# Two fused transformer blocks on one core: 128 weight loads issued by GpSimd in place of SyncE

## The chip, the cores and the metric

The kernel runs on one core of a Trainium2 chip, as one launch. Its time is the device time in microseconds (us) of that launch, the median of several runs. The core has five engines that matter here: TensorE (PE, matrix products, with its weight loads as PEld), VectorE (DVE), ScalarE (ACT), GpSimd (POOL) and SyncE (SP). Each engine carries out its own instructions in the order in which they stand in its stream, and an instruction at the head that waits holds back all that stand behind it. Sixteen DMA engines move data between the device memory and the on-chip memory; a transfer is issued by an instruction on one of the engines.

## The reference

Two transformer blocks on 256 tokens of width 2048 and batch 1, in f32. What this case touches is the first block's modulation: six vectors of 2048 numbers that come from one condition vector by one large weight matrix, `w_ada` (2048 x 12288 f32, 100.7 MB).

```python
cond = jax.nn.silu(c)
mod = cond @ w_ada[i] + b_ada[i]
shift1, scale1, gate1, shift2, scale2, gate2 = jnp.split(mod, N_MOD, axis=-1)
h = _modulate(_rms(x, norm1_w[i]), shift1, scale1).astype(x.dtype)
u, q, k, v = jnp.split(h @ w_in[i], splits, axis=-1)
y_ssm = _s5_mixer(u, ...)              # a scan over 256 steps, gelu, a gate
y_att = _dilated_attention(q, k, v, q_norm_w[i], k_norm_w[i])
mixed = jnp.concatenate([y_ssm, y_att], axis=-1) @ w_out[i]
x = x + gate1[:, None, :] * mixed
h2 = _modulate(_rms(x, norm2_w[i]), shift2, scale2).astype(x.dtype)
ffn = (jax.nn.silu(h2 @ w_ffn_gate[i]) * (h2 @ w_ffn_up[i])) @ w_ffn_down[i]
x = x + gate2[:, None, :] * ffn
```

A second block of another kind follows, with its own modulation weights (`ada_w_2`), attention over a context, and a layer that mixes by Fourier transforms. The change touches none of it.

## The kernel before, in words

**Weights as tiles of 512 KB.** Nearly all work is to stream weights past 256 tokens. A weight tile is 128 partitions x 2 x 512 f32 (512 KB), loaded into a buffer of the tag `raw`, of which there are five (`NRAW`). For a product, ACT writes the tile's upper part (`wh`, L177), DVE the rest (`wl<-raw,wh`, L178), three buffers each, and PE does three products for one: 12 matmuls for one tile of 256 weight rows, two token halves at a time (the "k2 step" of `gemm`). After each step `tick()` lets the side lanes go on.

**The lane `ada`.** The modulation is a vector times a matrix, done beside the rest by a generator, `ada_all`. A tile is loaded into a `raw` buffer, and DVE adds the tile times one condition value per partition to an accumulator (`acc<-raw,condT,acc`, L278, 128 x 1024). In order: the first gate (`row`, 32 tiles), the second shift and second scale (`cols1`, each 16 tiles through DVE by `ada_gen` and 16 through PE by `ada_quad`, which takes the raw tile itself as the moving operand), then the second gate (`row` again, 32 tiles), and after that the second block's vectors from `ada_w_2`. `ada_gen` issues its loads at L306, `ada_quad` at L353. The first block's first shift and scale come earlier, from another function with its own loads at L742 (64 of them), which no change concerns.

**What sets the order.** The lane's pace is given by hand (`rate["ada"]`), and `until("g1")`, `until("m2")`, `until("g2")` make it reach a point. In the feed-forward part:

```python
    rate["ada"] = 0.5                      # L1114: one lane step for two k2 steps
        if np_ == 0:
            lanes["ada"].until("g2")       # L1147: after the first half of the FFN
```

The program order is then rearranged per engine by the Tile framework's scheduler, which also decides which of the five `raw` buffers a tile gets and puts in the waits: a load waits until its buffer's last reader is done. All 192 loads of `w_ada` are SP instructions, as are the loads of the products' weights (L214, and L207 for tiles that PE uses unsplit); they stand in one stream and go through one hardware queue, q1. POOL has 12 memsets and no load.

Of the kernel before, what the change touches and what calls it, by code (L numbers as in the profile page):

```python
# [81 lines left out]
def kernel(ctx: ExitStack, tc: tile.TileContext, A, out):  # L82
    nc = tc.nc
    V, S, G, PE, SY = nc.vector, nc.scalar, nc.gpsimd, nc.tensor, nc.sync
# [14 lines left out]
    def uname(s):  # L99
        count[0] += 1  # L100
        return f"{s}_{count[0]}"
# [30 lines left out]
    def mm(o, l, r, start, stop):  # L132
        PE.matmul(o, l, r, start=start, stop=stop)  # L133
# [23 lines left out]
    def rsqrt(src, scale, shape, key="r"):  # L157

        w, y, t, yi = (small(shape, key + n, d) for n, d in (("w", F32), ("y", F32), ("t", F32), ("i", I32)))
        V.tensor_scalar(out=w, in0=src, scalar1=float(scale), scalar2=EPS, op0=ALU.mult, op1=ALU.add)  # L160
        V.tensor_scalar(out=yi, in0=w.bitcast(I32), scalar1=1, scalar2=None, op0=ALU.logical_shift_right)
        V.tensor_scalar(out=yi, in0=yi, scalar1=-1, scalar2=0x5F3759DF, op0=ALU.mult, op1=ALU.add)
        V.tensor_scalar(out=w, in0=w, scalar1=-0.5, scalar2=None, op0=ALU.mult)
        y0 = yi.bitcast(F32)
        for i in range(3):
            if shape[1] == 1:
                V.tensor_scalar(out=t, in0=y0, scalar1=y0, scalar2=w, op0=ALU.mult, op1=ALU.mult)
                V.tensor_scalar(out=y, in0=t, scalar1=1.5, scalar2=y0, op0=ALU.add, op1=ALU.mult)
            else:
                V.tensor_tensor(out=t, in0=y0, in1=y0, op=ALU.mult)  # L170
                V.tensor_tensor(out=t, in0=t, in1=w, op=ALU.mult)
                V.scalar_tensor_tensor(out=y, in0=t, scalar=1.5, in1=y0, op0=ALU.add, op1=ALU.mult)
            y0 = y
        return y
# [98 lines left out]
    def ada_add(acc, raw, vec, kk, first=False):  # L273
        c = condT[:, vec + kk:vec + kk + 1]
        if first:
            V.tensor_scalar(out=acc, in0=raw, scalar1=c, scalar2=None, op0=ALU.mult)
        else:
            V.scalar_tensor_tensor(out=acc, in0=raw, scalar=c, in1=acc, op0=ALU.mult, op1=ALU.add)  # L278
# [7 lines left out]
    def zipped(*gens):  # L286

        gens = list(gens)
        while gens:
            for g in list(gens):  # L290
                try:
                    yield next(g)
                except StopIteration:
                    gens.remove(g)

    def ada_gen(W, bc, col0, vecs, accs, row=False):

        bc = bc + col0 // 128
        if row:
            for j in range(8):  # L300
                S.activation(out=accs[0][:, j * 128:(j + 1) * 128], in_=ident, func=AF.Copy,
                             scale=bcol[:, bc + j:bc + j + 1])
        for kk in range(ND):
            raw = wp.tile([128, 2, 512], F32, name=uname("raw"), tag="raw", bufs=NRAW)
            rf = raw.rearrange("p k n -> p (k n)")
            SY.dma_start(rf, W[kk * 128:(kk + 1) * 128, col0:col0 + 1024])  # L306
            for a, v in zip(accs, vecs):
                ada_add(a, rf, v, kk, kk == 0 and not row)
            yield 1.0
# [37 lines left out]
    def ada_quad(b, W, r, c0, n, last):  # L347

        m = 1024 // n
        raws = []  # L350
        for q in range(0, 4, m):
            raw = wp.tile([128, m, n], F32, name=uname("raw"), tag="raw", bufs=NRAW)
            SY.dma_start(raw, W[(r + q) * 128:(r + q + m) * 128, c0:c0 + n].rearrange("(k p) n -> p k n", p=128))  # L353
            raws.append(raw)
            yield 1.0
        for j in range(4):
            mm(b[32 * j:32 * j + 32, 0:n], cz[:, r + j], raws[j // m][:, j % m], r == 0, last)

    def ada_pe(W, i, chunks, dst, add, mul=None):

        for c in chunks:
            b = ps_mm()
            for r in range(0, ND, 4):
                yield from ada_quad(b, W, r, i * D + c * 512, 512, r == ND - 4)
            cols = ada_turn(b, 512, 128)
            o = dst[:, c * 4:c * 4 + 4]
            bc = i * ND + c * 4
            V.tensor_reduce(out=o, in_=cols, axis=AX.X, op=ALU.add)
            V.scalar_tensor_tensor(out=o, in0=o, scalar=float(add), in1=bcol[:, bc:bc + 4], op0=ALU.add, op1=ALU.add)
            if mul is not None:  # L370
                V.tensor_tensor(out=o, in0=o, in1=colv[:, mul + c * 4:mul + c * 4 + 4], op=ALU.mult)
# [8 lines left out]
    w_ada = A["w_ada"][0]  # L380
    aw = A["ada_w_2"]

    def ada_all():
        def cols(W, bc, i, v, dst, add):

            accs = [ada_acc() for _ in range(2)]
            yield from zipped(*(ada_gen(W, bc, i * D + h * 1024, [v], [accs[h]]) for h in range(2)))
            ada_cols(accs, [(dst, 8 * h, bc + i * ND + 8 * h) for h in range(2)], add)

        def row(W, bc, i, v, dst):  # L390
            dst += [None] * 2
            accs = [ada_acc() for _ in range(2)]
            yield from zipped(*(ada_gen(W, bc, i * D + h * 1024, [v], [accs[h]], True) for h in range(2)))
            ada_row(accs, dst)

        def half(W, i, dst, add, mul):
            acc = ada_acc()
            yield from ada_gen(W, 0, i * D, [C_C], [acc])
            ada_cols([acc], [(dst, 0, i * ND)], add, mul)
# [432 lines left out]
    r = rsqrt(s1, 1.0 / D, [128, 2])  # L832
# [5 lines left out]
    for c0 in range(0, ND, 2):  # L838
        b = ps_tp()
        for c in range(2):  # L840
            for t in range(2):
                o = (c * 2 + t) * 128
                k = c0 + c
# [187 lines left out]
    for nt in range(4):  # L1031
        ps = gemm([(z, 0), (z, 1)], w_out, 0, 8, nt * 512, 512, stagger=3 * (nt == 3))
        for t in range(2):
# [8 lines left out]
            if nt == 3:  # L1042
                s1 = small([128, 1], "s1")
                V.tensor_reduce(out=s1, in_=ssq[t], axis=AX.X, op=ALU.add)
                r = rsqrt(s1, 1.0 / D, [128, 1])
# [689 lines left out]
```

## Time and profile before

| | |
|---|---|
| median of 3 runs | 2492.14 us (2489.64, 2492.14, 2492.82) |
| the profiled execution | 2486.17 us |
| its span, first to last instruction | 2484.4 us |
| mean granted TensorE clock | 0.983 |
| PE, DVE, ACT, POOL busy | 95%, 73%, 45%, 0% |
| memory traffic | 587.19 MB read, 237 GB/s over the span |
| loads of `w_ada`: L742, L306, L353 | 64, 96, 32, of 512 KB |
| their time in the span | L742 4.9 to 180.5 us, L306 191.7 to 707.0 us, L353 290.8 to 524.6 us |

The table is read in this way: PE is busy for nearly all of the span, so that another engine or a transfer costs time only where it makes PE wait. The stretch that holds loads of L306 and L353 goes from 191.7 to 707.0 us. In it lie the projections of the first block with its scan and attention (to about 453 us), the output projection and the second norm (to about 552 us), and that part of the feed-forward products beside which the second gate's tiles are loaded (to about 712 us).

### The profile page before, as it was taken

How to read it: one execution, taken by the hardware profiler on the slowest of the kernel's cores; microseconds unless marked ns; L12 is line 12 of the kernel's file. 1: busy time of each engine (PE TensorE's matmuls, PEld its weight loads, DVE VectorE, ACT ScalarE, POOL GpSimd, SP SyncE). 2: the span in 40 equal slices, each digit the busy share in tenths (PEclk: the TensorE clock that was granted, in tenths of full speed). 3: DMA queues.
4: the chain of work that ended last, by engine and by line, in shares of the span. 5: the costliest groups of instructions: out<-in, count | busy, mean ns of one | idle time of the engine just before them, and what ended most of it. 6: DMA issues, size and time to landing. Idle time of an engine off the chain costs nothing.

```text
span 2484.4 us, 30494 instructions
## 1 busy us (share of the span) xinstructions
PE 2352.2 (95%) x10855; PEld 1800.0 (72%) x10855; DVE 1810.1 (73%) x3054; ACT 1124.0 (45%) x1745; POOL 1.4 (0%) x12
## 2 busy tenths in 40 slices
PE   5899999989999999999999999999997999999997
PEld 3455554668887878778777888777776778888886
DVE  5877998787778899876778789646678655555557
ACT  3227752454444333344355455555435445444442
POOL 0000000000000000000000000000000000000000
PEclk9899999999999999999999999999998999999999
DMA  9888778768888878888877988624473765665664
GB/s 290 309 296 307 231 260 285 253 224 291 286 278 273 297 267 291 266 270 280 266 250 222 306 282 291 210 89 162 136 262 115 231 200 176 193 194 157 177 210 138
DMA packets 291538, 591.35 MB, mean 238 GB/s; under 512 B 33733, under 2 KB 56617, under 8 KB 291385
## 3 DMA queue, kind: packets, MB, share of 16 engines
q1 hardware_dynamic: 291384, 589.40, 73.1%
q8 instruction: 85, 1.39, 0.2%
q14 instruction: 69, 0.56, 0.1%
HBM read 587.19 MB, written 2.13 MB: 237 GB/s over the span
## 4 chain that ended last, share of the span: by engine, by line
PE 47%; DMA 22%; DVE 20%; issue 5%; ACT 4%; SPq 1%; DVEq 0%; ACTq 0%
PE mm L133 39%; DMA raw<-in_ada_w_dram 15%; DVE wl L178 6%; DVE acc L278 6%; PE at L133 4%; PE tp L133 2%; DMA raw<-in_w_in_attn_dram 2%; DMA raw<-in_w_ada_dram 2%; ACT ssm_us L663 1%; ACT wh L177 1%; DMA raw<-in_w_ffn_down_dram 1%; PE tp L189 1%; DVE ssm_h L684 1%; DVE ssm_tq L682 1%; DVE wa L278 1%
## 5 line engine op out<-in xcount | busy, mean ns | idle before, releaser
L133 PE MATMUL mm<-wh,s 128*128 128x512 f32 (+3 forms) x4768 | 1462.9, 386 | 2.3 <-ACT wh L177 2.1
L177 ACT CAST wh<-raw 128x1024 fp32r<-128x1024 f32 (+3 forms) x642 | 655.9, 1023 | 896.8 <-PE mm L133 669.9
L133 PEld LDWEIGHTS mm<-wh,s 128*128 128x128 f32 x4768 | 890.2, 189 | 181.1 <-issue 7.8
L178 DVE TENSOR_TENSOR wl<-raw,wh 128x1024 fp32r<-128x1024 f32 (+3 forms) x642 | 755.2, 1185 | 316.6 <-ACT wh L177 311.9
L133 PE MATMUL mm<-wl,s 128*128 128x512 f32 (+3 forms) x2384 | 920.4, 386 | 21.4 <-DVE wl L178 19.6
L278 DVE SCALAR_TENSOR_TENSOR acc<-raw,condT,acc 128x1024 f32<-128x1024 f32 (+2 forms) x413 | 477.7, 1164 | 208.8 <-DMA raw<-in_ada_w_dram 141.9
L133 PEld LDWEIGHTS mm<-wl,s 128*128 128x128 f32 x2384 | 450.5, 189 | 119.7 <-DVE wl L178 33.2
L133 PE MATMUL mm<-wh,sl 128*128 128x512 f32 x608 | 230.9, 475 | 5.1 <-ACT sl L753 2.8
L133 PEld LDWEIGHTS mm<-wh,sl 128*128 128x128 f32 x608 | 112.5, 191 | 68.2 <-issue 41.8
L133 PE MATMUL mm<-wl,sl 128*128 128x512 f32 x368 | 158.2, 494 | 2.6 <-DVE wl L178 2.5
L133 PEld LDWEIGHTS mm<-wl,sl 128*128 128x128 f32 x368 | 67.7, 189 | 52.8 <-issue 38.1
L684 DVE TENSOR_TENSOR ssm_h<-ssm_h,ssm_tq 128x128 f32<-128x128 f32 x256 | 73.2, 286 | 2.5 <-ACT ssm_h L673 1.0
L133 PE MATMUL at<-wl,sl 128*128 128x512 f32 x152 | 68.3, 597 | 1.1 <-DMA wl<-in_w_in_dram 0.5
L133 PE MATMUL tp<-wc,sl 128*128 128x128 f32 (+1 forms) x352 | 49.2, 293 | 18.8 <-ACT wc L837 15.1
L133 PEld LDWEIGHTS tp<-wc,sl 128*128 128x128 f32 x352 | 44.7, 198 | 29.0 <-ACT wc L837 15.4
L682 DVE TENSOR_TENSOR ssm_tq<-ssm_h,ssm_co 128x128 f32<-128x128 f32 x248 | 61.3, 286 | 1.8
L278 DVE SCALAR_TENSOR_TENSOR wa<-raw,condT,wa 128x512 f32<-128x512 f32 (+1 forms) x75 | 48.1, 641 | 11.6 <-DMA raw<-in_w_ada_dram 10.8
L133 PEld LDWEIGHTS at<-wl,sl 128*128 128x128 f32 x152 | 27.7, 190 | 38.7 <-issue 28.6
L133 PE MATMUL at<-s,s 128*128 128x512 f32 (+1 forms) x96 | 42.0, 616 | 3.7 <-ACT wd L1317 3.0
L133 PEld LDWEIGHTS at<-ssm_us,ssm_bl 128*128 128x128 f32 x256 | 30.6, 191 | 11.6 <-ACT ssm_h L673 5.7
L133 PE MATMUL at<-ssm_us,ssm_bl 128*128 128x128 f32 x256 | 34.0, 283 | 3.2 <-ACT ssm_h L673 1.4
L663 ACT COPY ssm_us<-sl 32x512 f32<-32x512 f32 (+3 forms) x56 | 34.4, 615 | 0.9
(330 smaller groups left out, 1588.8 us busy)
## 6 DMA issues: line engine op xcount, KB each, us to landing
raw<-in_w_ada_dram SPq DMA_DIRECT2D x192, 512.0 KB, 5.3
raw<-in_ada_w_dram SPq DMA_DIRECT2D x192, 512.0 KB, 4.8
raw<-in_w_in_fourier_dram SPq DMA_DIRECT2D x128, 512.0 KB, 4.2
raw<-in_w_ffn_gate_dram SPq DMA_DIRECT2D x88, 512.0 KB, 5.0
raw<-in_w_ffn_up_dram SPq DMA_DIRECT2D x88, 512.0 KB, 4.8
raw<-in_w_ffn_down_dram SPq DMA_DIRECT2D x88, 512.0 KB, 5.3
raw<-in_w_in_attn_dram SPq DMA_DIRECT2D x72, 512.0 KB, 5.1
raw<-in_w_out_fourier_dram SPq DMA_DIRECT2D x64, 512.0 KB, 4.2
```

Source lines behind the costliest of these rows:

```text
L133: PE.matmul(o, l, r, start=start, stop=stop)
L177: S.copy(hi, src)
L178: V.tensor_sub(lo, src, hi.bitcast(F32))
L189: PE.transpose(b[:, o:o + 128], src(c0 + c, t), ident)
L278: V.scalar_tensor_tensor(out=acc, in0=raw, scalar=c, in1=acc, op0=ALU.mult, op1=ALU.add)
L663: copy(d[:, :, z:NT], uT[half][32 * i:32 * i + 32, :, t0 + z - j:t0 + NT - j])
L682: V.tensor_tensor(out=tq, in0=prev[:, c:c + 1].to_broadcast([128, 2, 16, 4]), in1=cof[:, c].unsqueeze(3).to_broadcast([128, 2, 16, 4]), op ...
L684: V.tensor_tensor(out=cur, in0=cur, in1=tq, op=ALU.add)
```

## The change

A small function chooses the issuing engine by the weight matrix. The 96 loads of L306 whose matrix is `w_ada` and all 32 loads of L353 become POOL instructions; the later loads of L306, from `ada_w_2`, stay on SP. Size, buffers, number of buffers and the arithmetic stay. In the changed kernel's numbering all lines behind this place are four higher (L306 is L310, L353 is L357, L684 is L688).

```diff
+    def ada_queue(W):
+
+        return G if W is w_ada else SY
+
     def ada_gen(W, bc, col0, vecs, accs, row=False):
...
-            SY.dma_start(rf, W[kk * 128:(kk + 1) * 128, col0:col0 + 1024])
+            ada_queue(W).dma_start(rf, W[kk * 128:(kk + 1) * 128, col0:col0 + 1024])
...
     def ada_quad(b, W, r, c0, n, last):
...
-            SY.dma_start(raw, W[(r + q) * 128:(r + q + m) * 128, c0:c0 + n].rearrange("(k p) n -> p k n", p=128))
+            ada_queue(W).dma_start(raw, W[(r + q) * 128:(r + q + m) * 128, c0:c0 + n].rearrange("(k p) n -> p k n", p=128))
```

Since the scheduler sets each engine's order, more moves than the 128 rows. First SP in the feed-forward part, before: a load of `w_ada` stands between each two loads of the products' weights.

```order
L306 DMA raw_1167_4904<-in_w_ada_dram 128x1024 [waits DMAHW2_49,DVE_49]
L214 DMA raw_1168_4907<-in_w_ffn_gate_dram 128x2x512 [waits DMAHW0_49,DVE_49]
L214 DMA raw_1171_4925<-in_w_ffn_gate_dram 128x2x512 [waits DMAHW1_49,DVE_49]
L306 DMA raw_1174_4943<-in_w_ada_dram 128x1024 [waits DMAHW5_49,DVE_49]
L214 DMA raw_1175_4946<-in_w_ffn_gate_dram 128x2x512 [waits DMAHW3_49,DVE_49]
L214 DMA raw_1182_4970<-in_w_ffn_up_dram 128x2x512 [waits DMAHW4_49,DVE_49]
```

SP at the same place in the changed kernel holds the products' loads alone.

```order
L214 DMA raw_1168_4907<-in_w_ffn_gate_dram 128x2x512 [waits DMAHW7_49,DVE_49]
L214 DMA raw_1171_4925<-in_w_ffn_gate_dram 128x2x512 [waits DMAHW0_49,DVE_49]
L214 DMA raw_1175_4946<-in_w_ffn_gate_dram 128x2x512 [waits DMAHW1_49,DVE_49]
L214 DMA raw_1182_4970<-in_w_ffn_up_dram 128x2x512 [waits DMAHW2_49,DVE_49]
L214 DMA raw_1186_4991<-in_w_ffn_up_dram 128x2x512 [waits DMAHW3_49,DVE_49]
```

And POOL at that place in the changed kernel (before, it had nothing there).

```order
L310 DMA raw_1160_4865<-in_w_ada_dram 128x1024 [waits DMASW1_49,DMASW0_49,DVE_49]
L310 DMA raw_1167_4904<-in_w_ada_dram 128x1024 [waits DMASW1_49,DVE_49]
L310 DMA raw_1174_4943<-in_w_ada_dram 128x1024 [waits DMASW3_49,DMASW2_49,DVE_49]
L310 DMA raw_1185_4988<-in_w_ada_dram 128x1024 [waits DMASW4_49,DMASW3_49,DVE_49]
L310 DMA raw_1192_5027<-in_w_ada_dram 128x1024 [waits DMASW4_49,DVE_49]
L310 DMA raw_1199_5066<-in_w_ada_dram 128x1024 [waits DMASW5_49,DVE_49]
```

DMASW marks a transfer issued by POOL, DMAHW one issued by SP, DVE the reader. Each POOL load waits for DVE and for a POOL transfer just before it in the stream, which means that it goes into the `raw` buffer that the last `w_ada` tile had; the products' loads wait for SP transfers alone and go round in the other four.

The second place is DVE where the norm of q begins (L160), in the first projections. Before, the rows ahead of it are these.

```order
L278 SCALAR_TENSOR_TENSOR acc_279_1372<-raw_467_2112,condT_80,acc_279_1372 128x1024
L682 TENSOR_TENSOR ssm_tq_323_1527<-ssm_h_253_1221,ssm_co_562 128x128
L682 TENSOR_TENSOR ssm_tq_324_1530<-ssm_h_253_1221,ssm_co_562 128x128
L684 TENSOR_TENSOR ssm_h_253_1221<-ssm_h_253_1221,ssm_tq_323_1527 128x32x4
L278 SCALAR_TENSOR_TENSOR acc_280_1373<-raw_497_2206,condT_80,acc_280_1373 128x1024
L160 TENSOR_SCALAR rhw_298_1437<-ssh_293_1428 128x4
```

In the changed kernel the same place reads so, and the tile that came last before the norm (raw_497_2206) stands 26 rows further up.

```order
L278 SCALAR_TENSOR_TENSOR acc_279_1372<-raw_579_2512,condT_80,acc_279_1372 128x1024
L686 TENSOR_TENSOR ssm_tq_291_1420<-ssm_h_253_1221,ssm_co_562 128x128
L686 TENSOR_TENSOR ssm_tq_292_1423<-ssm_h_253_1221,ssm_co_562 128x128
L688 TENSOR_TENSOR ssm_h_253_1221<-ssm_h_253_1221,ssm_tq_291_1420 128x32x4
L278 SCALAR_TENSOR_TENSOR acc_280_1373<-raw_580_2515,condT_80,acc_280_1373 128x1024
L688 TENSOR_TENSOR ssm_h_253_1221<-ssm_h_253_1221,ssm_tq_292_1423 128x32x4
L160 TENSOR_SCALAR rhw_298_1437<-ssh_293_1428 128x4
```

Eight more tiles of `w_ada` (raw_508_2238 to raw_580_2515) are added up ahead of the norm, and fewer steps of the scan (`ssm_tq`, `ssm_h`) stand there: the scan has come to ssm_tq_292 in place of ssm_tq_324. By the scan's last step both orders have the same number of `w_ada` tiles behind them, 220 accumulations. From the glu stage on PE's order is the same in both.

## Rows read from the trace of the kernel before

**Rows 1.** First page: busy time (share) of two engines; the DMA queue

```profile
PE 2352.2 (95%) x10855; PEld 1800.0 (72%) x10855; DVE 1810.1 (73%) x3054; ACT 1124.0 (45%) x1745; POOL 1.4 (0%) x12
q1 hardware_dynamic: 291384, 589.40, 73.1%
```

**Rows 2.** Windows: length; busy PE, PEld, DVE, ACT, POOL; clock, DMA share, GB/s

```profile
183.00:255.00 72.00, 68.94 (x277) 40.29 (x276) 53.88 (x121) 49.80 (x108) 0.37 (x3) 1.00 0.89 316
255.00:424.00 169.00, 165.84 (x818) 85.48 (x819) 156.15 (x612) 86.42 (x210) 0.21 (x1) 1.00 0.75 250
424.00:453.00 29.00, 25.65 (x78) 9.08 (x76) 27.97 (x90) 5.94 (x9) 0.00 (x0) 1.00 0.87 305
453.00:552.00 99.00, 91.23 (x450) 69.53 (x451) 74.25 (x118) 53.46 (x85) 0.00 (x0) 0.93 0.73 236
552.00:712.00 160.00, 160.00 (x721) 132.75 (x720) 114.13 (x106) 72.44 (x80) 0.00 (x0) 1.00 0.85 281
```

**Rows 3.** Chain of the feed-forward stretch: start, length, what

```profile
597.68 43.55 PE mm L133 x192
641.23 0.87 PE tp L189 x8
```

**Rows 4.** Waits of DVE and of SP, 552 to 712 us: total, times, longest

```profile
DVE acc L278 <- DMA raw<-in_w_ada_dram: 31.2, 25, 2.4
SPq L306 <- DVE acc L278: 32.4, 26, 1.4
```

**Rows 5.** Timeline of DVE, feed-forward part: start, busy, what, idle before

```profile
639.93 1.28 DVE L278 SCALAR_TENSOR_TENSOR acc<-raw,condT,acc 128x1024 f32<-128x1024 f32 x1
...
646.57 1.28 DVE L278 SCALAR_TENSOR_TENSOR acc<-raw,condT,acc 128x1024 f32<-128x1024 f32 x1 [1.80 <-DMA raw<-in_w_ada_dram]
647.77 2.35 DVE L178 TENSOR_TENSOR wl<-raw,wh 128x1024 fp32r<-128x1024 f32 x2
```

**Rows 6.** Timeline of SP at the same place

```profile
641.24 0.34 SPq L306 DMA_DIRECT2D raw<-in_w_ada_dram  x1
...
647.89 0.34 SPq L306 DMA_DIRECT2D raw<-in_w_ada_dram  x1
```

**Rows 7.** The w_ada tiles, 552 to 712 us: issues, first and last, landing

```profile
L306 SPq DMA_DIRECT2D raw<-in_w_ada_dram x28: 340/341/341, 559.1 to 707.0; - x28
...
DMA to landing us min/median/max: 3.4/4.0/5.3
```

**Rows 8.** DMA of that stretch: issues, KB, median us to landing

```profile
raw<-in_w_ffn_up_dram SPq DMA_DIRECT2D x32, 512.0 KB, 4.9
...
raw<-in_w_ffn_gate_dram SPq DMA_DIRECT2D x26, 512.0 KB, 4.8
```

**Rows 9.** All w_ada tiles of the span

```profile
DMA to landing us min/median/max: 3.4/5.3/9.8
```

**Rows 10.** Timeline of SP, first projections

```profile
191.68 9.54 SPq L306 DMA_DIRECT2D raw<-in_w_ada_dram  x6
202.99 0.38 SPq L207 DMA_DIRECT2D wh<-in_w_in_dram  x1
```

**Rows 11.** Timeline of DVE, first projections

```profile
213.15 1.28 DVE L278 SCALAR_TENSOR_TENSOR acc<-raw,condT,acc 128x1024 f32<-128x1024 f32 x1 [3.73 <-DMA raw<-in_w_ada_dram]
...
238.53 0.49 DVE L682 TENSOR_TENSOR ssm_tq<-ssm_h,ssm_co 128x128 f32<-128x128 f32 x2
238.95 0.61 DVE L684 TENSOR_TENSOR ssm_h<-ssm_h,ssm_tq 128x128 f32<-128x128 f32 x2
...
250.04 0.17 DVE L160 TENSOR_SCALAR rhw<-ssh 128x4 f32<-128x4 f32 x1 [2.56 <-ACT jk L933]
```

**Rows 12.** Timeline of PE behind the norm of q

```profile
255.55 0.33 PE L189 MATMUL tp<-ident,sl 128*128 128x128 f32 x1 [1.30 <-ACT sl L937]
```

**Rows 13.** Timeline of DVE around the second norm

```profile
528.19 1.28 DVE L278 SCALAR_TENSOR_TENSOR acc<-raw,condT,acc 128x1024 f32<-128x1024 f32 x1 [0.48 <-DMA raw<-in_w_ada_dram]
...
538.08 1.67 DVE L1050 TENSOR_SCALAR sl<-sl,ry 128x512 f32<-128x512 f32 x4
```

## The prediction, made before the changed kernel ran

> **What bounds the kernel now.** I read the page first. PE is busy for 95% of the span, POOL for 1.4 us, and every load goes through one hardware queue [rows 1]. So I look for places where a load of `w_ada` stands before PE, and I take windows over the stretch that holds the moved loads (from 191.7 to 707.0 us). In the windows PE's idle time is the length less its busy time: 3.1, 3.2, 3.4, 7.8 and, in the feed-forward part, 0.0 us, 17.4 us in all [rows 2]. This is the most that the change could ever win there, with every wait of PE gone. The DMA share of 0.73 to 0.89 says that the engines of the transfers are well used, but not full.
>
> The feed-forward part looks safe (PE 160.00 of 160.00 us), and it is not. The chain there is PE alone: 192 matmuls in 43.55 us, then 0.87 us of transposes [rows 3]. Twelve matmuls are one k2 step, so this is 16 steps, 2.72 us each; with the transposes two steps take (43.55 + 0.87) / 8 = 5.55 us. The lane does one tile of `w_ada` in two steps. The waits of DVE show that it already stands for these tiles, 25 times for 31.2 us, up to 2.4 us; and SP's wait to issue one is mostly for DVE's accumulation, 26 times [rows 4]. The two timelines show the loop that this is. The accumulation begins at 639.93 and takes 1.28 us [rows 5]; the next tile is issued at 641.24, 0.03 us later [rows 6]; its accumulation begins at 646.57, after 1.80 us of waiting, and ends at 647.85 [rows 5]; the next issue is at 647.89 [rows 6]. So a `w_ada` tile goes into the buffer of the one before it. One turn is landing + 1.28 + 0.03 us. With the median landing of 4.0 us that is 5.31 us, against PE's 5.55: a slack of 0.24 us. The 28 issues from 559.1 to 707.0 are 147.9 / 27 = 5.48 us apart [rows 7], which is what a loop tied to PE gives.
>
> In the first projections the picture is another. SP issues six `w_ada` loads in a block of 9.54 us from 191.68, and a load of `w_in` behind them leaves only at 202.99 [rows 10]. DVE waits once for 3.73 us for a `w_ada` tile, runs scan steps between accumulations, and begins the norm of q at 250.04 after 2.56 us of idle time [rows 11]; PE comes to it at 255.55, after 1.30 us [rows 12].
>
> **The change part by part.** *Removed from SP:* 128 issues. In the feed-forward stretch they are 28 of 0.34 us, 9.5 us [rows 7]. I cost this at nothing: PE waits for nothing there [rows 2].
>
> *Added to POOL:* the same 128 issues, on an engine with 1.4 us of work [rows 1]. What a transfer that POOL issues takes to land is not in this trace, where POOL issues none. So I bound it by rows. From below: the shortest landing of the stretch, 3.4 us [rows 7]. From above: the longest of any `w_ada` tile, 9.8 us [rows 9]. Between lie 4.0 (the tiles of today, mostly alone in the queue when they go out) and 4.9 and 4.8 us, the medians of the products' loads beside them, of equal size [rows 8]. I take 4.9: the order shows that SP no longer puts `w_ada` into its own stream but goes on with the products' loads, so that a tile of POOL's will usually share the DMA engines with one of these; and the products' loads, of equal size and issued beside others, are the nearest rows there are to that.
>
> *The feed-forward loop.* The order leaves a `w_ada` tile in the buffer of the one before, so the loop stays. One turn with 4.9 us is 4.9 + 1.31 = 6.21 us, 0.66 more than PE's 5.55; over 27 turns 17.8 us. DVE's order is fixed, and behind the waiting accumulation stand two `wl` of the products (647.77, 2.35 us for both [rows 5]), so PE waits for these. What PE has in hand when the loop falls behind I take as one k2 step, 2.7 us. Term: **+15 us**. With 3.4 us the turn is 4.71 and the term 0 (PE sets the pace); with 5.3, the longest of this stretch today, 1.06 x 27 - 2.7 = +26; with 9.8, 5.56 x 27 - 2.7 = +147. The point from which it costs anything is a landing of 4.24 us, and 0.1 us more to use up the step in hand.
>
> The Trainium skill, "DMA: Bandwidth & Descriptors", section "Issuing engines are not separate DMA queues", speaks against a term of this size: all transfers run on the same 16 engines whoever issues them, and another issuer saves only the sequencer's time to issue. By that alone the landing stays at 4.0 us and the sum is the rival of no change below. The same page's "Latency and other measured facts" puts the first byte of a POOL-issued transfer at about 1 us against some 0.6 us; my estimate from this is 4.4 us of landing, 0.16 x 27 - 2.7, or +2 us in place of +15. No run here shows either so far.
>
> *The first projections.* The order puts eight more accumulations ahead of the norm of q, 8 x 1.28 = 10.2 us of DVE at most, and some five pairs of scan steps fewer, each (0.49 + 0.61) / 2 = 0.55 us, 2.8 us [rows 11]. DVE's 2.56 us of idle time before the norm takes up part of the 7.4 us that are left, so the norm begins up to 4.9 us later, and PE, which comes to it in order and already waits 1.30 us [rows 12], would wait about that much more. Later the scan has fewer accumulations between its steps; both orders have 220 of them behind the last step, and PE has 3.4 us of idle time at the scan's end [rows 2] that can shrink. With nothing given back, and DVE waiting 0.9 us longer at six of the tiles ahead of the norm, it is 4.9 + 6 x 0.9 = +10; with all given back and the block on SP gone (202.99 would come some 9 us earlier [rows 10], the wait of 3.73 falls away [rows 11]) it is -5. I take **+3 us**, nearer the middle.
>
> *Around the second norm* DVE waits 0.48 us for a tile at 528.19, ahead of the norm's steps [rows 13]. A landing 0.9 us longer makes it wait that much more, **+1 us**; ends 0 and +3.
>
> *Sum:* 15 + 3 + 1 = +19 us. On the profiled execution, 2486.2 us, that is 2505 us; the median of the timed runs is 2492.1, 6 us above it, and so I forecast **2511 us**. With landings of 4.6 to 5.5 us the loop gives (0.36 x 27 - 2.7) = +7 to (1.26 x 27 - 2.7) = +31, so the forecast's own range is 2500 to 2530.
>
> **Rivals.** *No change, 2492 us.* POOL's transfers land as SP's do, at 4.24 us or less, and the first projections give back what they lose. For it: 4.0 us leaves room, POOL has no other work. Against it: the slack is 0.24 us in 5.55.
>
> *Faster, 2483 us.* SP's stream no longer stops for the accumulations. The six loads of 9.54 us no longer stand before the loads of `w_in`, the tile that DVE waited 3.73 us for is there in time, and the scan is done sooner; landing stays below 4.24 us, the point from which it no longer holds. The price: half of PE's idle time of 17.4 us, -9 us. For it: rows 10. Against it: PE's idle time is spread over many small waits, and waiting for a load is hardly among them where I show them (it waits for the norm at 255.55 [rows 12]).
>
> *Much slower, 2552 us.* POOL prepares its transfers only where DVE leaves it room. DVE is busy 114 of 160 us there [rows 2], and one stretch of two `wl` is 2.35 us [rows 5]; held back by this, the landing is 4.0 + 2.35 = 6.35 us, the turn 7.66, and the loop 2.11 x 27 - 2.7 = +54; with the other terms and their own share +60. Against it: nothing of the trace shows DVE holding POOL back. The Trainium skill, "SBUF — State Buffer", section "SBUF: two separate sides", says that POOL cannot write the descriptors of its transfers while DVE runs in a mode that takes both ports, and gives 3.1 us in place of 0.62 for one small transfer. This trace would show such an operation by a short time for its size: 512 elements in 0.42 us at 538.08 (1.67 us for four [rows 13]) against 1024 in 1.28 us for the accumulation [rows 5]. In the feed-forward loop I see the slow kind, so the rule, as far as this goes, would leave the loop alone; by its figure the term would be an estimated +58 us.
>
> *The norm of q alone, 2497 us.* The landing is harmless, but DVE's new order in the first projections costs its 4.9 us of PE.
>
> **How the numbers follow.** A measurement of this kernel tells about 0.2%, 5 us, from no change. Forecast 0.50 (slower 0.48, the same 0.02: a landing of 4.5); no change 0.20 (same 0.17, slower 0.02, faster 0.01); faster 0.14 (faster 0.12, same 0.02); much slower 0.08; the norm of q alone 0.08 (slower 0.05, same 0.03). In all: faster 0.13, same 0.24, slower 0.63. The range that holds eight in ten leaves out most of the faster case below, and the much slower case above: 2487 to 2540.
>
> **What would show it right or wrong.** In the profile after, POOL's queue has 128 issues, and their landing in the feed-forward part is near 4.9 us; the issues there are 6.2 us apart and not 5.48; PE has idle time there, some 15 us, put down to DVE's `wl`; DVE's wait for `w_ada` tiles grows beyond 31.2 us. The norm of q begins a few us later against the scan. If the 28 issues are still 5.5 us apart, the main step is wrong, and the result must lie within some 5 us of 2492; if PE's idle time between 183 and 552 us has shrunk, the faster rival was the case.

## The result and the profile after

The changed kernel takes 2525.07 us (median of 4 runs, 2522.12 to 2530.68) against 2490.89 us of the kernel before beside it; the ratio is 1.0141, 95% interval [1.0118, 1.0164], which is 29 to 41 us slower. Forecast were 2511 us, slower, and a range of 2487 to 2540: direction and range held, and the forecast had a little more than half of the loss (19 of 34 us). The working below shows that the term I counted most on came near its size, but by another way than I had thought, and that some 13 us of the loss sit in a stretch to which I gave next to nothing.

The page after shows the move itself: POOL has 76.3 us of work [rows 1], and a second queue carries 67 MB.

```profile
PE 2363.7 (94%) x10855; PEld 1808.1 (72%) x10855; DVE 1808.9 (72%) x3054; ACT 1123.4 (45%) x1745; POOL 76.3 (3%) x140
q1 hardware_dynamic: 268856, 522.28, 64.4%
q0 software_dynamic: 18432, 67.12, 7.8%
```

The windows that [rows 2] cut, in the kernel after (length; busy PE, PEld, DVE, ACT, POOL; clock, DMA share, GB/s):

```profile
183.00:255.00 72.00, 64.21 (x257) 38.01 (x256) 52.38 (x77) 40.40 (x72) 16.85 (x34) 0.93 0.90 329
255.00:424.00 169.00, 160.98 (x792) 86.06 (x791) 147.09 (x623) 94.57 (x244) 26.36 (x43) 0.98 0.66 221
424.00:453.00 29.00, 29.00 (x92) 11.15 (x91) 25.08 (x82) 2.93 (x5) 6.90 (x11) 1.00 0.83 285
453.00:552.00 99.00, 89.25 (x419) 63.45 (x417) 68.05 (x104) 40.44 (x52) 8.94 (x14) 0.95 0.70 224
552.00:712.00 160.00, 147.95 (x649) 119.38 (x649) 110.60 (x140) 75.94 (x103) 13.55 (x26) 0.96 0.78 261
```

PE's idle time is 7.8, 8.0, 0.0, 9.8 and 12.1 us here, against 3.1, 3.2, 3.4, 7.8 and 0.0, and the granted clock is below 1.00 in four of the five windows, where it was below 1.00 in one. The windows stand at fixed times, and from the norm of q on everything comes 10 to 20 us later here, so that the last window holds a part of the second norm too. The loss is thus in at least three places. To find them I followed the same instructions through both traces:

| the same instruction | before | after | later by |
|---|---|---|---|
| PE's first transposes of the scan's input (L627, now L631) | 122.6 | 123.4 | 0.8 |
| PE's first transpose behind the norm of q (L189) | 255.55 | 265.75 | 10.2 |
| PE's first transpose of the second norm (L457, now L461) | 535.93 | 556.59 | 20.7 |
| the last `w_ada` issue | 707.05 | 740.82 | 33.8 |
| end of the span | 2484.4 | 2521.0 | 36.6 |

**The feed-forward part: 13 us.** The 28 issues that answer to [rows 7], DVE's waits that answer to [rows 4], and PE's waits:

```profile
L310 POOL DMA_DIRECT2D raw<-in_w_ada_dram x28: 528/531/531, 580.2 to 740.8; - x28
...
DMA to landing us min/median/max: 3.7/4.0/6.7
```

```profile
DVE acc L278 <- DMA raw<-in_w_ada_dram: 56.3, 28, 4.8
```

```profile
PE mm L133 <- DVE wl L178: 7.9, 5, 2.9
```

The turn is (740.82 - 580.20) / 27 = 5.95 us in place of 5.48, and PE, which waited for nothing there, waits five times for `wl`, 7.9 us in all. The rest of the 12.7 us is PE being busy longer over the 27 turns (152.7 us in place of 147.9, at a granted clock of 0.99 in place of 1.00). But the median landing is 4.0 us as before, not 4.9. What has changed stands in the timelines. First POOL, then DVE (start, length, what, idle before):

```profile
603.17 0.53 POOL L310 DMA_DIRECT2D raw<-in_w_ada_dram  x1 [5.09 <-DVE acc L278]
608.48 0.53 POOL L310 DMA_DIRECT2D raw<-in_w_ada_dram  x1 [4.79 <-DVE acc L278]
...
642.78 0.53 POOL L310 DMA_DIRECT2D raw<-in_w_ada_dram  x1 [6.23 <-DVE wl L178]
650.54 0.53 POOL L310 DMA_DIRECT2D raw<-in_w_ada_dram  x1 [7.23 <-DVE acc L278]
```

```profile
601.59 1.28 DVE L278 SCALAR_TENSOR_TENSOR acc<-raw,condT,acc 128x1024 f32<-128x1024 f32 x1 [2.07 <-DMA raw<-in_w_ada_dram]
602.79 2.35 DVE L178 TENSOR_TENSOR wl<-raw,wh 128x1024 fp32r<-128x1024 f32 x2
606.90 1.29 DVE L278 SCALAR_TENSOR_TENSOR acc<-raw,condT,acc 128x1024 f32<-128x1024 f32 x1 [1.75 <-DMA raw<-in_w_ada_dram]
...
641.27 3.49 DVE L178 TENSOR_TENSOR wl<-raw,wh 128x1024 fp32r<-128x1024 f32 x3
648.96 1.28 DVE L278 SCALAR_TENSOR_TENSOR acc<-raw,condT,acc 128x1024 f32<-128x1024 f32 x1 [4.21 <-DMA raw<-in_w_ada_dram]
```

The accumulation ends at 601.59 + 1.28 = 602.87, and POOL issues at 603.17: 0.30 us later, where SP took 0.03 [rows 5, 6]. The shortest landing is 3.7 us against 3.4 [rows 7]. So the shortest turn was 3.4 + 1.28 + 0.03 = 4.71 us and is 3.7 + 1.28 + 0.30 = 5.28. PE's two steps take 5.55, so even now such a turn keeps up with PE.

The time is lost where a `w_ada` tile takes the buffer of a product's tile. These are the waits for the buffer of all 28 loads, before (SP) and after (POOL); a wait that a `wl` ends tells of such a change of buffer:

```profile
SPq L306 <- DVE acc L278: 32.4, 26, 1.4
SPq L306 <- DVE wl L178: 2.6, 2, 1.9
```

```profile
POOL raw L310 <- DVE acc L278: 123.2, 23, 7.8
POOL raw L310 <- DVE wl L178: 32.0, 5, 8.9
```

Before, only the first two of the 28 loads change the buffer. In the changed kernel the scheduler's new order has three more changes, at 642.78, 692.15 and 740.82; the part of the order that is shown ahead of the prediction has none of them. The tiles that leave at these changes land late (6.2 to 6.7 us), and the next turn is long too: the tile of 642.78 takes 6.2 us, DVE stands 4.21 us, and the next load leaves after 7.76 us. The seven turns that end or begin with a change take 48.4 us, which is 9.6 more than seven times PE's 5.55; the other 20 take 5.61 each, close to PE's pace. So most of the loss stands at the changes of buffer, and not in a longer turn through one buffer. A long turn could be made good by the next ones at up to 0.84 us each before, and at 0.27 now; how much of the loss comes of that is argued and not shown, since no run has these changes of buffer with loads by SP and whole accumulations.

**Up to the norm of q: 10 us.** POOL is not held back by SP's order, and its first three loads of the first gate leave at 183.38, 188.02 and 190.99, where SP sent the first at 191.68, behind the loads of `w_in` [rows 10]. A tile of `w_in` that SP issued at 187.79 before and at 188.35 now is cast on ACT 5.5 us later before and 10.0 us later now. SP and ACT, before:

```profile
187.79 0.50 SPq L214 DMA_DIRECT2D raw<-in_w_in_dram  x1
...
193.28 1.04 ACT L177 CAST wh<-raw 128x1024 fp32r<-128x1024 f32 x1 [16.19 <-DMA raw<-in_w_in_dram]
```

After:

```profile
188.35 0.47 SPq L214 DMA_DIRECT2D raw<-in_w_in_dram  x1
...
198.32 1.05 ACT L177 CAST wh<-raw 128x1024 fp32r<-128x1024 f32 x1 [20.91 <-DMA raw<-in_w_in_dram]
```

DVE waits for this cast, and behind that in DVE's order stand the steps that PE needs. DVE, then PE:

```profile
199.40 1.23 DVE L178 TENSOR_TENSOR wl<-raw,wh 128x1024 fp32r<-128x1024 f32 x1 [7.39 <-ACT wh L177]
```

```profile
202.47 6.64 PE L133 MATMUL at<-wh,sl 128*128 128x512 f32 x8 [2.37 <-DVE col L752]
...
226.07 3.37 PE L133 MATMUL mm<-wh,sl 128*128 128x512 f32 x4 [2.75 <-DMA wh<-in_w_in_dram]
...
265.75 0.33 PE L189 MATMUL tp<-ident,sl 128*128 128x128 f32 x1 [2.25 <-ACT sl L941]
```

PE waits 2.37 us. The eight matmuls behind it take 6.64 us, while eight of the kind take 3.60 later (208.95): the granted clock is 0.55 from 202.40 to 209.10 us, near the level of 1.2 GHz, after the stretch from 199.10 to 202.40 us in which PE was busy for 1.00 of 3.30 us; in the kernel before it is 1.00 (2.4 GHz) at this place (198.40 to 205.00 us). Then PE waits 2.75 us for a `w_in` tile. In the stretch from 165 to 262 us the median landing of `w_in` loads went from 5.6 to 8.4 us. Before, then after:

```profile
DMA to landing us min/median/max: 3.7/5.6/9.3
```

```profile
DMA to landing us min/median/max: 4.6/8.4/13.9
```

The eight extra accumulations ahead of the norm stand behind 240 us in DVE's order, and the 10 us are there sooner: PE's first matmuls of the scan's input (`at<-ssm_us,ssm_bl`) begin at 229.28 in place of 218.56.

**Between the norm of q and the second norm: another 10 us.** At 352.54 DVE waits 5.71 us for a `w_ada` tile, whose load POOL could issue only when PE had ended a product with a tile that it reads itself (344.13), and the scan ends so late that PE stands 7.28 us before its last product. POOL, DVE, then PE:

```profile
344.13 0.56 POOL L310 DMA_DIRECT2D raw<-in_w_ada_dram  x1 [1.62 <-PE mm L133]
```

```profile
352.54 1.29 DVE L278 SCALAR_TENSOR_TENSOR acc<-raw,condT,acc 128x1024 f32<-128x1024 f32 x1 [5.71 <-DMA raw<-in_w_ada_dram]
```

```profile
465.52 3.67 PE L133 MATMUL at<-ssm_h,ssm_cl 128*32 128x128 f32 x64 [7.28 <-DVE ssm_h L688]
```

Of these 10.5 us only 1.7 lie before the scan's end. The other 8.8 lie between the scan's end and the second norm, where PE has 421 matmuls in place of 398: it waited for the scan (10.3 us in three places) and has work left that was done by then in the kernel before.

### The profile page after: what moved, and what is told of

The parts are those of the page before. It is cut to its first block, busy times and chain, and to the rows that moved or that the text cites. A ratio compares the mean times of both kernels' runs of the same rounds, so it can differ in the third digit from the quotient of the medians.

```text
span 2521.0 us, 30572 instructions
## 1 busy us (share of the span) xinstructions
PE 2363.7 (94%) x10855; PEld 1808.1 (72%) x10855; DVE 1808.9 (72%) x3054; ACT 1123.4 (45%) x1745; POOL 76.3 (3%) x140
## 4 chain that ended last, share of the span: by engine, by line
PE 32%; DMA 18%; DVE 15%; issue 5%; ACT 2%; DVEq 0%; SPq 0%; ACTq 0%; POOLq 0%
PE mm L133 27%; DMA raw<-in_ada_w_dram 15%; DVE wl L178 6%; DVE acc L278 5%; PE at L133 2%; PE tp L133 1%; DMA raw<-in_w_in_attn_dram 1%; ACT wh L177 1%; DMA raw<-in_w_ffn_down_dram 1%; DVE sl L1510 0%; DVE sl L1513 0%; PE tp L189 0%; PE tp L1335 0%; DVE wb L1163 0%; DMA raw<-in_w_ffn_gate_dram 0%
## 5 line engine op out<-in xcount | busy, mean ns | idle before, releaser
L688 DVE TENSOR_TENSOR ssm_h<-ssm_h,ssm_tq 128x128 f32<-128x128 f32 x256 | 72.7, 284 | 3.0 <-ACT ssm_h L677 1.6
L310 POOL DMA_DIRECT2D raw<-in_w_ada_dram x96 | 52.0, 542 | 394.9 <-DVE acc L278 148.4
```

The costliest lines, as they stand in the source:

```text
L310: ada_queue(W).dma_start(rf, W[kk * 128:(kk + 1) * 128, col0:col0 + 1024])
L688: V.tensor_tensor(out=cur, in0=cur, in1=tq, op=ALU.add)
```

## The experiments

The ten runs come in three batches; a run's time stands against that of before on the same chip. Since the first 123 us, where nothing is changed, differ by up to 5 us from profile to profile, and the part behind the last moved load, also unchanged, by up to 11 us, I compare stretches of the profiles and not their ends.

### One group of loads at a time (e1 to e4, e8)

The issuing function gets the column, and with it the vector (`i` is 2 for the first gate, 3 and 4 for the second shift and scale, 5 for the second gate):

```diff
-        return G if W is w_ada else SY
+        return G if W is w_ada and col0 // D == 2 else SY          # e1, e8
+        return G if W is w_ada and col0 // D in (3, 4) else SY     # e2
+        return G if W is w_ada and col0 // D == 5 else SY          # e3
+        return G if W is w_ada and col0 // D > 2 else SY           # e4
```

e1: 

> Only the 32 loads of the first gate are issued by POOL; second shift, second scale and second gate stay on SP. Theory A (two separate places): the first gate's loads leave from 183 us instead of 191.7, among the loads of w_in, and PE stands 10 us later at the norm of q and about 20 us later at the second norm; so +15 to +21 us over before, none of it in the feed-forward part (its w_ada issues 5.5 us apart again). Rival B (every POOL load is a little slower, wherever it is): the loss goes by the number of loads, 32 of 128 of 34 us, +8.5 us.

e2: 

> Only the 64 loads of the second shift and second scale (half of them through PE) are issued by POOL. Theory A: 0 to +3 us, since there are neither w_in loads to be overtaken nor the feed-forward loop. Rival B: half the loads, +17 us.

e3: 

> Only the 32 loads of the second gate are issued by POOL. Theory A: +13 us, all in the feed-forward part, where PE falls idle at the two or three places at which a w_ada tile takes a buffer from a product's tile; the time at the second norm is that of before (535.9 us). Rival B: +8.5 us, spread evenly over the part.

e4: 

> All but the first gate's loads are issued by POOL (96 of 128). Theory A: the sum of the two runs before, +13 to +16 us. Rival B: three quarters, +26 us.

| on POOL | us | before | ratio, 95% interval |
|---|---|---|---|
| e1, first gate | 2493.96 | 2489.89 | 1.0015 [1.0000, 1.0030] |
| e2, second shift and scale | 2504.84 | 2489.89 | 1.0063 [1.0048, 1.0078] |
| e3, second gate | 2499.15 | 2489.89 | 1.0038 [1.0024, 1.0051] |
| e4, all but the first gate | 2520.22 | 2489.89 | 1.0122 [1.0107, 1.0137] |

Theory A missed: the first gate costs 4 us and not 15 to 21, the second shift and scale, to which it gave 0 to 3, cost 15, and e4, to which it gave 13 to 16, costs 30. Only for the second gate is it near, 9 us for 13, with the second norm where it said (538.4 us, of which 4.0 come from the first 123 us). The totals are near to rival B (8.5, 17, 8.5, 26 us). But the traces don't show its even spread either: in e3, where PE's order is that of before, PE's waits are four, 6.0 us in all, and its 27 turns are like those of the changed kernel: 8.5 us lost in the seven turns at changes of buffer, 5.55 us for each of the others. Timed alone, the parts do not add up: 4 + 15 + 9 = 28 us against 34 for the whole change, and 15 + 9 = 24 against 30 for e4. In e4's trace the 27 turns take 14.9 us more than before, in e3's 10.5; why is open.

e8: 

> The first gate's loads alone on POOL, once more with a profile: in the first profile PE was 10 us late at the norm of q, yet the timed runs gave only +4 us. Expected if the 10 us are given back by the scan's end: PE 8 to 10 us late at the norm of q, at most 4 to 5 us late at the second norm (540 us). If the first profile was typical: 9 us or more there.

The second profile of e1's kernel has its norm of q at 267.21 (11.7 us later than before, of which 2.2 came from the first 123 us) and the second norm at 544.96 (9.0 later, 6.9 without the 2.2). In the first profile the second norm was 8.9 us later without the first 123 us. So some 3 us are given back by then, fewer than expected. The timed loss of 4 us has an interval from 0 to 7.5 us, which holds 6.9, and both profiled executions were long ones (2508.18 and 2501.80 us against a median of 2493.96); whether more is given back behind the second norm stays open.

### The second shift and scale, in halves and in one stream (e5, e6, e9)

e5 moves only the tiles that PE reads itself (L353), e6 only those that DVE adds up (L306 for `i` 3 and 4). e9 puts all weight loads of the first block, from the first gate to the second norm, on POOL:

```diff
+    Q = [SY]                       # e9; every raw, wh and wl load is issued by Q[0]
...
     rate["ada"] = T["ada"]
+    Q[0] = G
...
     lanes["ada"].until("m2")
+    Q[0] = SY
```

e5: 

> Of the second shift and second scale only the 32 tiles that PE reads itself are issued by POOL, the 32 that DVE adds up stay on SP. Theory H (POOL's one stream is held at its head: tiles that wait for PE and tiles that wait for DVE stand in turn in it): alone, either half costs little, 0 to +4 us, and PE's wait for such tiles (4.5 us in three places when both halves are on POOL) is gone. Rival L (each POOL transfer comes some 0.5 us later than SP's, and DVE or PE pays for each): half of the 15 us, +7 us, for each half.

e6: 

> The other half: of the second shift and second scale only the 32 tiles that DVE adds up are issued by POOL. Theory H: 0 to +4 us. Rival L: +7 us. A third reading (the scheduler's new order of DVE and PE is what costs, not the transfers) gives no number for this run beforehand; it would show as PE's idle time at the scan's end without a longer wait of DVE for w_ada tiles than the 7.1 us of before.

e9: 

> From the first gate's loads to the second norm every weight load of the first block (w_in, w_out, w_glu and w_ada) is issued by POOL, in one stream again; the feed-forward part is as before, all on SP. Theory S (SP's one stream was also an order of delivery, and two streams let loads that are not yet needed take the DMA engines from those that are): with one stream the loss before the second norm is gone, the norm at 536 to 541 us, total 0 to +5 us. Rival L (each turn through a buffer is longer by POOL's later start and longer issue, 0.3 + 0.2 to 0.35 us): the second norm still 10 us or more late, total +10 to +20 us.

Measured: e5 2509.28 against 2489.90, 1.0081 [1.0049, 1.0113]; e6 2505.92, 1.0061 [1.0030, 1.0091]; e9 2510.21 against 2490.70, 1.0070 [1.0052, 1.0089]. Each half alone costs as much as both: theory H and rival L, which gave a half 0 to 4 or 7 us, both miss. In e6 DVE's waits for `w_ada` tiles grew, so the sign that was set for the third reading, a late scan without longer waits, was not seen. And one stream doesn't cure it, so theory S falls as the main cause: e9's loss lies in the range of rival L. Up to the norm of q, though, e9 bears theory S out. There the median landing of `w_in` loads is 4.6 us (8.4 after, 9.7 and 8.4 in the two profiles of e1's kernel), and DVE comes to the norm 3.7 us later in place of 9.3, both without the first 123 us:

```profile
DMA to landing us min/median/max: 4.0/4.6/8.9
```

The rest of e9's loss is 8.4 us from the norm of q to the scan's end and 4.1 us from there to the second norm.

What the stretch is bound by, the traces do show. These are windows from the norm of q (DVE's first L160) to the end of the scan (length, busy PE, PEld, DVE, ...), and DVE's wait for `w_ada` tiles in them (us, times, longest). Before:

```profile
250.04:453.61 203.57, 195.83 (x905) 96.23 (x903) 189.69 (x737) 97.58 (x241) 0.21 (x1) 1.00 0.77 261
```

```profile
DVE acc L278 <- DMA raw<-in_w_ada_dram: 3.1, 6, 0.7
```

e5:

```profile
249.52:472.72 223.20, 205.11 (x930) 103.73 (x928) 193.44 (x739) 99.68 (x243) 20.53 (x29) 0.96 0.72 245
```

```profile
DVE acc L278 <- DMA raw<-in_w_ada_dram: 23.3, 13, 5.4
```

e9:

```profile
258.88:470.81 211.93, 200.66 (x905) 98.61 (x904) 190.13 (x740) 96.97 (x241) 63.39 (x98) 0.96 0.74 252
```

```profile
DVE acc L279 <- DMA raw<-in_w_ada_dram: 9.5, 5, 6.2
```

DVE is busy 189.7 of 203.6 us before, and PE 195.8: here DVE has hardly more room than PE. Of the chain of work that ended last, loads of `w_ada` hold 6% of this stretch before, 13% in e9, 21% in e6, 25% in e2 and 28% in e5. With each kernel's wait at L276 added (the first accumulation of a vector, 0.6 to 2.6 us):

| kernel | streams that carry the tiles and the products' loads | DVE busy | its wait for `w_ada` | length |
|---|---|---|---|---|
| before | one (SP) | 189.7 | 4.2 | 203.6 |
| e9 | one (POOL) | 190.1 | 11.1 | 211.9 |
| e2 | `w_ada` on POOL, the rest on SP | 193.3 | 15.1 | 216.3 |
| e6 | `w_ada` in both, the rest on SP | 193.2 | 19.0 | 218.7 |
| e5 | `w_ada` in both, the rest on SP | 193.4 | 24.2 | 223.2 |
| after | `w_ada` on POOL, the rest on SP | 181.5 | 16.1 | 205.3 |
| e8 | as before; first gate earlier, on POOL | 178.6 | 1.7 | 190.9 |

Wait and length grow together: e9 +6.9 and +8.4, e2 +10.9 and +12.7, e6 +14.8 and +15.1, e5 +20.0 and +19.6. The last two rows have less DVE work in the stretch because the order has put accumulations ahead of the norm of q; the changed kernel pays for its wait of 16.1 us out of that. What the 64 loads cost it is read against e8, which has the first gate on POOL as well: from the norm of q to the second norm e8 takes 2.6 us less than before and the changed kernel 10.5 more, so 13 us, as in e2 (12.7). Less work of DVE alone brings little, though: e8's stretch to the scan's end is 12.7 us shorter, and 10.1 us of that are lost again before the second norm, since PE still has its work to do.

So it is shown that late `w_ada` tiles at DVE make the loss of this stretch in e2, e5, e6 and e9. Why they are late is shown in part. Their transfers are not longer as a whole: the median landing of `w_ada` tiles in the stretch is 5.3 us before and 5.1 to 5.5 in the other kernels that lose. The longest waits of e9 (6.2 us) and of the changed kernel (5.7) are for tiles that could be issued only when PE had ended a product with a tile that it reads itself. In e9:

```profile
342.47 0.58 POOL L307 DMA_DIRECT2D raw<-in_w_ada_dram  x1 [1.62 <-PE mm L134]
```

In e9 nothing is split and 6.9 us are there all the same: POOL issues slower (0.58 and 0.71 us against 0.34 and 0.37) and starts later, and these tiles too go round in a few buffers. The rest is larger in the kernels in which loads that share the five buffers are split between two streams; this is an order of four numbers, one profile each, and I have not taken the two apart.

### The turn of the feed-forward part (e7, e10)

e7 moves the second gate's loads as e3 does and adds up half of each tile; e10 leaves all loads on SP and does each accumulation in four pieces:

```diff
+                h = 512 if W is w_ada and col0 // D == 5 else 1024     # e7
+                ada_add(a[:, 0:h], rf[:, 0:h], v, kk, kk == 0 and not row)
...
+                w = 256 if W is w_ada and col0 // D == 5 else 1024     # e10
+                for o in range(0, 1024, w):
+                    ada_add(a[:, o:o + w], rf[:, o:o + w], v, kk, kk == 0 and not row)
```

e7: 

> The second gate's 32 loads on POOL, as in the run that cost +9 us, but DVE adds up only the left 512 of each tile's 1024 columns (the right half of the second gate is left out; all loads stay). The accumulation is 0.69 us in place of 1.28, and by the order the scheduler then gives a w_ada tile another buffer than the last one's. Theory A for the feed-forward part (the turn of landing, accumulation and issue through one buffer is as long as PE's two steps, so nothing lost at a change of buffers is made good): within 2 us of before, turns after a long one shorter than 5.2 us. Rival (POOL's transfers are late by themselves, or take the products' loads' bandwidth): still +6 us or more.

e10: 

> All loads on SP as before. The second gate's accumulation of a tile is done in four pieces of 256 columns, about 2.0 us in place of 1.28; nothing is left out. Theory A for the feed-forward part (the turn of one buffer, landing + accumulation + start of the next load, is what binds): the turn goes from 5.3 to 6.0 us, 0.45 above PE's 5.55, so some 28 x 0.45 = 12 us less the 2.7 of the step in hand: +8 to +12 us, without any transfer by POOL. Rival (the loss of the second gate's run comes of POOL's transfers sharing the DMA engines): 0 to +2 us, since DVE is busy only 114 of 160 us there.

e7 took 2542.95 against 2489.90 us, 1.0219 [1.0186, 1.0251]: 53 us slower, where I expected 2 at most. The expectation missed, and the turn itself explains why: I had not asked whose buffer it was that the tile now takes. So e7 does not test a shorter turn; it has the change of buffer in nearly every turn. The timelines of POOL and DVE in e7:

```profile
600.47 0.53 POOL L310 DMA_DIRECT2D raw<-in_w_ada_dram  x1 [6.68 <-DVE wl L178]
608.16 0.53 POOL L310 DMA_DIRECT2D raw<-in_w_ada_dram  x1 [7.16 <-DVE wl L178]
```

```profile
598.96 2.35 DVE L178 TENSOR_TENSOR wl<-raw,wh 128x1024 fp32r<-128x1024 f32 x2
601.23 1.28 DVE L1139 TENSOR_TENSOR wa<-wa,mm 128x512 f32<-128x512 f32 x2
605.97 0.75 DVE L278 SCALAR_TENSOR_TENSOR acc<-raw,condT,acc 128x512 f32<-128x512 f32 x1 [3.47 <-DMA raw<-in_w_ada_dram]
606.64 2.35 DVE L178 TENSOR_TENSOR wl<-raw,wh 128x1024 fp32r<-128x1024 f32 x2
```

A `w_ada` tile now waits for the `wl` of a product's tile, and this `wl` stands in DVE's order behind the accumulation of the tile before. The turn is landing 5.5 (600.47 to 605.97), accumulation 0.75, one `wl` 1.2 and POOL's start 0.3: 7.7 us. Over all turns it is 7.56, which by the prediction's sum is 27 x (7.56 - 5.55) - 2.7 = 52 us; 53 were timed. PE's wait for `wl` is 38.3 us in 22 places there.

e10 took 2495.90 against 2490.70 us, 1.0021 [1.0008, 1.0034]: +5 us (2 to 8), below the 8 to 12 expected and above the rival's 0 to 2. But it is not the turn I had meant. The scheduler put `wl` between the pieces and gave the tiles other buffers, so that 25 of the 28 loads are freed by a product's `wl`, as in e7. DVE, then SP:

```profile
661.24 0.88 DVE L278 SCALAR_TENSOR_TENSOR acc<-raw,condT,acc 128x256 f32<-128x256 f32 x2 [2.11 <-DMA raw<-in_w_ada_dram]
662.04 1.22 DVE L178 TENSOR_TENSOR wl<-raw,wh 128x1024 fp32r<-128x1024 f32 x1
663.18 0.88 DVE L278 SCALAR_TENSOR_TENSOR acc<-raw,condT,acc 128x256 f32<-128x256 f32 x2
```

```profile
663.29 0.34 SPq L306 DMA_DIRECT2D raw<-in_w_ada_dram  x1
```

The load at 663.29 leaves as this `wl` ends (662.04 + 1.22 = 663.26), with two pieces of the last tile still to be done. The turn came to 5.81 us, not 6.0; by the same sum this is 27 x 0.26 - 2.7 = +4 us, and PE waits 3.6 us for `wl` in six places, where it waited for nothing. No transfer by POOL is in it, so changes of buffer that make the turn longer cost time with SP as well. What a longer turn through one and the same buffer costs is tested by no run.

The turn in all kernels, from the last 28 issues:

| kernel | issued by | the buffer is freed by | turn |
|---|---|---|---|
| before | SP | the last accumulation (26 of 28) | 5.48 |
| e1, e8, e2, e5, e6, e9 | SP | the last accumulation (26 of 28) | 5.50 to 5.59 |
| e10 | SP | a product's `wl` (25 of 28) | 5.81 |
| e3, after, e4 | POOL | the last accumulation (22 or 23 of 28) | 5.87, 5.95, 6.03 |
| e7 | POOL | a product's `wl` (26 of 28) | 7.56 |

No version ran faster than the kernel before.

## Why the prediction was right in sign and short in size

*The feed-forward loop, +15.* The place and the size held: by turns it measured 12.7 us in the changed kernel, and +9 timed alone (e3). That the size came near is in good part luck, for the way was another. I had said that the order leaves a `w_ada` tile in the buffer of the one before, and that each of the 27 turns is 0.66 us too long by a landing of 4.9 us. The median landing stayed at 4.0 us, and POOL starts 0.3 us after the buffer is free, which no row of before could show; with these the turn is 4.0 + 1.28 + 0.30 = 5.58 us, 0.03 more than PE's pace, and my sum gives nothing. The loss came at three changes of buffer, 9.6 us in seven turns, where the prediction had none. Of the signs I had set, PE's idle time (7.9 us for 15), the distance of the issues (5.95 us for 6.2) and DVE's waits (56.3 us, beyond 31.2) came, the landing did not.

What the Trainium skill, "DMA: Bandwidth & Descriptors", section "Latency and other measured facts", would have added to the landing, some 0.4 us, is near to the 0.3 by which the shortest landing grew; the median did not grow. The Trainium skill's section "Issuing engines are not separate DMA queues" on the same page agrees with the unchanged median landing here. That another issuer saves the time to issue and does no more, as it says, is not what these runs show: POOL also starts later after its wait, 0.30 us against 0.03.

*The first projections, +3.* Right in sign and place, but for another reason and too small: 9.3 us up to the norm, of which e8 gives 2.6 back by the second norm. I had DVE's eight extra accumulations before the norm; what made PE 10 us late there was that POOL's loads leave 8 us earlier and get in among the loads of `w_in`. The block on SP's stream, which I had booked as a possible gain, held no load of `w_in` back. The one at 202.99 waited for PE, whose matmuls on its buffer end at 201.08 + 1.88 = 202.96:

```profile
201.08 1.88 PE L133 MATMUL at<-wh,sl 128*128 128x512 f32 x4
```

So the lower end of this term and the faster rival rested in part on a wrong reading. The block was rather a protection: it kept loads with time to spare behind those that were needed. Alone the first gate costs +4 us.

*The step that failed* is the second half of that term, "later the scan has fewer accumulations between its steps", with PE's idle time at the scan's end as what it could be paid from. I priced the second shift and scale at nothing but a place in this give-back, and gave the second norm +1. From the norm of q to the scan's end DVE has hardly more room than PE, 189.7 of 203.6 us busy; that row I had in [rows 2] as 156.15 of 169 and 27.97 of 29 us, and I read only PE's column. There the 64 loads cost 13 us by the traces and +15 us timed alone (e2). By the trace of the changed kernel the loss is 12.7 (feed-forward part), 9.3 less 2.6 (first gate) and 13 us (second shift and scale), where I had 15, 3 and 1.

*The rivals.* No change and faster are out by the interval. DVE holding POOL back was not seen: this rival had a landing of 6.35 us, and the median is 4.0; and POOL's issue is 528 to 531 ns long at every one of the loop's 28 issues, whatever DVE did. The Trainium skill's rule in "SBUF — State Buffer", section "SBUF: two separate sides", speaks of a mode of DVE that takes both ports. By the sign that the prediction set, a short time for the size, the loop has no such operation (1.22 and 1.28 us for 1024 elements), so no run here tests it.

## What to carry to other kernels

Before a load is moved to another issuer, look for the buffer it goes round in: reader's end, start of the issue, landing, reader. Then look in the new order for the places where it takes a buffer that another kind of tile had: here three such changes in 28 loads cost most of what the feed-forward part lost, and a loop that changes the buffer in nearly every turn cost 53 us (e7). A load held behind others in one stream is also kept from overtaking them: ask what it will compete with when it is free. And ask of each stretch how much room each engine has, and not only PE: where DVE was busy for 93% of the time, its longer waits came back nearly in full (e6: 14.8 us of wait, 15.1 us of length).

## What the runs showed of the hardware that was not expected

A load issued by POOL starts 0.30 us after the end of the reader it waits for, against 0.03 us for SP, and the issue itself takes mostly 0.53 to 0.58 us for 128x1024 (0.70 to 0.72 for 128x2x512) against 0.34 (0.37). Between issue and landing there is hardly a difference: median 4.0 us for both in the feed-forward part. Moving half of a sequence of loads that share buffers was no cheaper than moving all of it: e5 and e6, which moved 32 loads, cost 19 and 16 us (intervals 12 to 28 and 7 to 23), e2, which moved 64, 15 (12 to 19). Loads on a second queue that leave earlier made others land later: the median landing of `w_in` went from 5.6 to 8.4 us, and was 4.6 with all loads in one POOL stream (e9).
